# Longer distances, later splits and another block order on a TensorE stream of three blocks (Trainium2, one core)

## The chip, the cores and the metric

The kernel runs on one core of one Trainium2 chip, in one launch. The metric is the device time in microseconds (us), from three runs; one further execution is profiled. Five engines share the work, each with a program order of its own: TensorE (PE in the rows, with PEld for its weight loads), VectorE (DVE), ScalarE (ACT), GpSimd (POOL), and SyncE (SP), which issues most DMAs. TensorE's clock has two levels here, 1.2 and 2.4 GHz; the profile states which one was granted.

## The reference, cut to what matters

256 tokens of width 1024 in float32 go through an even layer, an odd layer and a second block with a mixer and a feed-forward part. Heads are kept 128 or 64 wide.

```python
# even: gated short convolution beside a gated delta rule with 8 heads
g = -exp(a_log) * softplus(a_raw + dt_bias)            # per token and head
decay = exp(where(incl, gc[..., :, None] - gc[..., None, :], -inf))     # gc = cumsum(g) in a chunk
low = where(strict, (kb @ k.T) * decay, 0)
u, w = triangular_solve(low + I, [v * beta, kb * exp(gc)])
o = rms_norm(gated_delta_rule(...), gdn_norm_g) * silu(z_b)
s = concatenate([y_a, o]) @ w_out                      # 16 blocks of 128 rows
# odd: hgrn2 recurrence, s = (rms_norm(o) * silu(z)) @ w_out
# end of both layers, the gate:
x = layer_norm(ALPHA * x + s)
x = x + (p @ w_pl) * sigmoid(x @ w_pl_gate)
# mixer of the second block
y_fox, y_moba = softmax attention (6 + 6 heads of 64, with decay or slopes as bias)
h_ml = mlstm(...)                                      # 4 heads of 64
y_ml = rms(h_ml) * ml_h_g * sigmoid(mo)
x = x + g1 * (concatenate([y_fox, y_ml, y_moba]) @ w_out)
# then the feed-forward part: x + g2 * ((silu(gate) * up) @ w_down)
```

## The kernel before, in words

**Weights.** All large weights lie in one DRAM stream in the order in which TensorE takes them, cut into chunks of 1 MB (16 blocks of 128x128, `BLK`). `Stream` loads a chunk into one of three `raw` buffers (a DMA on SyncE's queue) and splits each half of it in two: ScalarE casts the high part (`hi<-raw`, 128x1024), VectorE subtracts it (`lo<-raw,hi`). There are six buffers each of hi and lo, three chunks in all. `Stream.take` hands TensorE one block after the other, and `fetch` is called from it at each half chunk for the half two chunks ahead. A block costs three matmuls: hi by the high part of the activations, hi by their low part, lo by the high part (`products`, and `dense_tok` for the mixer's values with 512 columns).

**Order.** The order of TensorE's program is written by hand. Everything that isn't a stream of weight blocks (heads of the delta rule, attention pairs, norms) is a generator in a `Side` queue. After every second block, `products` calls `side.tick(0.65)`; a generator that has yielded a number d is resumed d later on that clock, so d sets how many dense blocks stand on TensorE between two steps of a head (0.65 is two blocks: six matmuls of 256 columns, or three of 512 in `dense_tok`). The other engines' orders are made by the framework's scheduler from the same program; an instruction waits in its engine's queue for everything ahead of it. `issue_after` (the `late` argument) keeps a split behind a named instruction in that order.

**Steps that the change touches.**
- `gates` of the delta rule: for each head two tiles `gm` (VectorE scales the constant `gt` by a column of g), read by TensorE with the constant `tri`; ScalarE's exponential gives `la`.
- `gdn_out`, the step of a head: levels m16 and m32 of the inverse with the tiles T, U, MT and X, and at the end the norm, `o` scaled by ScalarE, `yield 4.0`, two transposes of `o`, and y with its split `yh`, `yl`, which the layer's out product reads.
- `out_plan`: the order of (k, m) blocks of an out product; the last four k go bank by bank (a bank is two m). When a bank is full, x is updated and its transposes for the layer norm are queued.
- `layer_tail`'s gate, `GATE_PLANS`: six columns m, then column 6, then column 7. When a bank is full, a tanh, a product (`q<-q,f` in the odd layer) and the add (`x<-x,q`) follow; in the odd layer `fold` transposes x for the next norm.
- the mixer's attention pairs (`pr` is the softmax, transposed after `yield 4.95`) and its `mlstm` (`lo_` is its output, transposed after `yield 4.0`; this `lo_` isn't a weight's `lo`).

Of the kernel before, what the change touches and what calls it, by code (L numbers as in the profile page):

```python
# [6 lines left out]
F32 = mybir.dt.float32  # L7
# [4 lines left out]
ALU = mybir.AluOpType  # L12
# [4 lines left out]
P = 128  # L17
# [13 lines left out]
BLK = 16  # L31
# [29 lines left out]
def out_plan(ks, tail):  # L61


    n = len(ks) - tail
    return [(k, m) for k in ks[:n] for m in range(8)] + \
        [(k, m) for j in range(4) for k in ks[n:] for m in (2 * j, 2 * j + 1)]

# [2 lines left out]
QK_BLOCKS = [0, 1, 6, 7, 2, 3, 8, 9, 4, 5, 10, 11]  # L72

OUT_PLANS = [out_plan([0, 1, 2, 3, 4, 5, 6, 8, 9, 10, 11, 7, 12, 13, 14, 15], 4),
             out_plan(list(range(16)), 4), out_plan([3, 4, 0, 1, 2, 5, 6, 7], 4)]
DOWN_GROUPS = [[0, 1], [2, 3], [4, 5], [6], [7]]

# [28 lines left out]
class Side:  # L106
# [3 lines left out]
    def __init__(self):  # L110
        self.now, self.qs = 0.0, {}
# [36 lines left out]
class Stream:  # L148
# [2 lines left out]

    def __init__(self, net, dram):
        self.net, self.dram, self.n, self.have, self.pos = net, dram, dram.shape[0], {}, 0
        self.late = ()
        self.fetch(0)

    def fetch(self, c, halves=(0, 1), late=()):
        if c < self.n:
            if 0 in halves:
                self.have[c] = self.net.load_chunk(self.dram[c])  # L160
            for h in halves:
                self.net.split_half(self.have[c], h, late)

    def take(self, width=1):
        c, b = divmod(self.pos, BLK)
        self.pos += width
        if c == 0 or c < TWO:
            if b == (0 if c else BLK // 2):
                self.fetch(c + 1, late=() if c else None)
        elif c == TWO:  # L170
            if b % (BLK // 2) == 0:
                self.fetch(c + 1 + b // (BLK // 2))
        else:
            if b % (BLK // 2) == 0:
                self.fetch(c + 2, (b // (BLK // 2),), self.late)
            if b >= BLK // 2:
                self.late = ()
        if b == 0:
            self.have.pop(c - 1, None)
        _, hi, lo = self.have[c]  # L180
        h, j = divmod(b, BLK // 2)
        s = slice(j * P, (j + width) * P)
        return hi[h][:, s], lo[h][:, s]
# [16 lines left out]
class Net:  # L200
# [222 lines left out]
    def gdn_gates(self):  # L423
        nc, ep, pr = self.nc, self.ep, self.prm
        out = self.ps("m")
        mul = self.narrow(self.wba, out)
        for k in range(KT):
            mul(k)
        yield 1.0
        bv = yield from self.to_tokens(out, self.e1, "t1", 0.0)  # L430
        tl = lambda n, w=16: ep.tile([P, w], F32, name="gg_" + n)
        v3 = lambda t: t.rearrange("p (h n) -> p h n", h=2)
        self.beta = tl("beta")
        asp = tl("asp")
        self.tt(v3(asp), bv[:, :, 8:], pr["dt_bias"].unsqueeze(1).to_broadcast([P, 2, 8]), ALU.add)
        th = tl("th")
        self.act(v3(th), bv[:, :, :8], AF.Tanh, scale=0.5)
        self.ts(self.beta, th, 0.5, 0.5)
        sp = self.softplus(self.e1, asp, 16)
        ea = tl("ea", 8)  # L440
        self.act(ea, pr["a_log"], AF.Exp)
        g = tl("g")
        self.stt(v3(g), v3(sp), -1.0, ea.unsqueeze(1).to_broadcast([P, 2, 8]))
        yield 3.5
        q = self.ps("m")
        self.mm(q[:, :16], self.c("tri"), g)
        self.mm(q[:, 16:32], self.c("gt"), g)
        self.eg = ep.tile([P, 32], F32, name="eg")
        self.act(self.eg, q[:, :32], AF.Exp)

        for h in range(0, GH, 2):
            la = ep.tile([P, 2, 2, 2, P], F32, tag="la", bufs=GH // 2, name=self.nm("la"))
            d = self.ps("m")
            for e in range(2):
                gm = self.e1.tile([P, 2, P], F32, tag="gm", bufs=2, name=self.nm("gm"))
                for s in range(2):
                    self.ts(gm[:, s], self.c("gt"), v3(g)[:, s, h + e:h + e + 1])
                    o = d[:, (2 * e + s) * P:(2 * e + s + 1) * P]
                    self.mm(o, gm[:, s], self.c("tri"), stop=False)
                    self.mm(o, self.bf["id"], self.bf["neg"], start=False)  # L460
            self.act(la[:, :, :, 1], d.rearrange("p (e a t) -> p e a t", e=2, a=2), AF.Exp)
            self.la += [la[:, 0], la[:, 1]]
# [143 lines left out]
    def gdn_out(self, h, s, ti, at):  # L606
        nc, ep = self.nc, self.ep
# [13 lines left out]
        for lev in ("m16", "m32"):  # L621
            mt = t2([P, 2, P], "MT")
            self.tt(mt, la[:, :, 0], self.c(lev).unsqueeze(1).to_broadcast([P, 2, P]))
            yield 1.3
            p = self.ps("m")
            for a_ in range(2):
                self.mm(p[:, a_ * P:(a_ + 1) * P], mt[:, a_], t[:, a_])
            self.act(xs, sp(p[:, :T]), AF.Copy)
            yield 0.65
            p2 = self.ps("m")  # L630
            for a_ in range(2):
                if lev == "m32":
                    self.mm(p2[:, a_ * P:(a_ + 1) * P], u[:, a_], xs[:, a_])
                self.mm(p2[:, T + a_ * P:T + (a_ + 1) * P], xs[:, a_], u[:, a_])
            v = p2.rearrange("p (w a t) -> p w a t", w=2, a=2)
            if lev == "m32":
                self.tt(t, t, v[:, 0], ALU.subtract)
            self.tt(u, u, v[:, 1], ALU.subtract)
            if lev == "m16":
                nc.vector.transpose(flat(t), flat(u))  # L640
# [50 lines left out]
        self.stt(sr, sr, P ** -0.5, rr[:, 2:4])  # L691
        for a_ in range(2):
            self.act(o[:, a_], o[:, a_], AF.Copy, scale=sr[:, a_:a_ + 1])
        yield 4.0
        pt = self.ps("m")
        for a_ in range(2):
            self.tr(pt[:, a_ * P:(a_ + 1) * P], o[:, a_])
# [24 lines left out]
    def out_ln_gate(self, i, y, done, lp):  # L722
        nc, xp = self.nc, self.xp
# [29 lines left out]
        for j in range(4):  # L753
            b = self.ps()
# [9 lines left out]
            nh, nl = self.xs()  # L764
        for plan in GATE_PLANS:
            first = plan[0][1]
            n = min(len({m for _, m in plan}), 2)
            bs = [self.ps() for _ in range(3 if n == 2 else 1)]

            def gated(q):  # L770
                j, b = first + 2 * q, bs[q]
                th, pj = gth[:, j // 2 % 2, j % 2:j % 2 + n], pw[j // 4][:, j % 4:j % 4 + n]
                v = x[:, j:j + n]
                self.act(th, b[:, :n * T].rearrange("p (m t) -> p m t", m=n), AF.Tanh, scale=0.5)
                self.stt(th, th, 1.0, pj, ALU.add, ALU.mult)
                self.tt(v, v, th, ALU.add)
                if i == 0:

                    for hs in (slice(0, P), slice(T - 1, P - 1, -1)):
                        self.split(nh[:, j:j + n, hs], nl[:, j:j + n, hs], v[:, :, min(hs.start, P):][:, :, :P])  # L780
                else:
                    self.fold(j, n)
            self.products((xh, xl), [(k, m - first) for k, m in plan], [(b, c) for b in bs for c in (0, T)], self.normed, gated)

    def ln_stats(self, x, j, st):
        yield 1.0
        tp = self.ps("m")
        for a_ in range(2):
            for m in range(2):
                self.tr(tp[:, (2 * a_ + m) * P:(2 * a_ + m + 1) * P], x[:, 2 * j + m, a_ * P:(a_ + 1) * P])  # L790
        for a_ in range(2):
            self.nc.vector.bn_stats(st[:, a_, j], tp[:, a_ * T:(a_ + 1) * T])
        self.banks += 1
# [427 lines left out]
    def softmax_pair(self, p_, kq, vs, yh, yl):  # L1221

        nc, ep = self.nc, self.ep
# [3 lines left out]
        for e in range(2):  # L1227
            h = 2 * p_ + e
            rows = slice(64 * e, 64 * e + 64)
            q, k = kq[rows, p_], kq[rows, 6 + p_]  # L1230
# [10 lines left out]
            s = self.ps("m")  # L1241
# [11 lines left out]
            pts.append(pr)  # L1253
            if e == 0:
                yield 0.65
        yield 4.95
        pt2 = []
        for e in range(2):

# [9 lines left out]
        for e in range(2):  # L1269
            h = 2 * p_ + e  # L1270
# [6 lines left out]
        n = p_ if p_ < 3 else p_ + 2  # L1277
# [34 lines left out]
    def lstm(self, vs, yh, yl):  # L1312
        nc, ep = self.nc, self.ep
# [6 lines left out]
        for h in range(4):  # L1320
            rows = slice(64 * (h % 2), 64 * (h % 2) + 64)
            q, k = self.mqk[rows, h // 2], self.mqk[rows, 2 + h // 2]
            e = self.ps("m")
            for a_ in range(2):
                c = slice(2 * a_ * P, (2 * a_ + 1) * P)
# [6 lines left out]
            s = self.ps("m")  # L1332
# [6 lines left out]
        for a_ in range(2):  # L1339
            pn = self.ps("m")  # L1340
            for h in range(4):
                c = slice(65 * h, 65 * h + 65)
# [5 lines left out]
            v = pn[:, :260].rearrange("p (h d) -> p h d", d=65)  # L1348
# [11 lines left out]
            self.tt(o, o, rs.unsqueeze(2).to_broadcast([P, 4, 64]))  # L1360
            os.append(o)
            yield 0.65
        yield 4.0
        pt = self.ps("m")
        for a_ in range(2):
            for j in range(2):
# [132 lines left out]
```

## Time and profile before

| | us |
|---|---|
| median of three runs (lowest, highest) | 1008.61 (1007.92, 1011.15) |
| the profiled execution's own time | 1007.96 |
| its span from the first to the last instruction | 1006.1 |
| TensorE busy | 978.8 (97%) |
| VectorE busy | 759.1 (75%) |
| ScalarE busy | 554.2 (55%) |
| mean granted clock of TensorE | 0.996 of 2.4 GHz |

A busy share is an average over stages. Matmuls are pipelined, so the duration of one in a row is longer than the distance to the start of the next. "[0.71 <-DVE x L322]" behind a row means that the engine sat idle for 0.71 us before it and what ended that.

### The profile page before, as it was taken

To read this page: it belongs to the slowest core of one execution; us is meant where nothing else is said; L and a number is where in the kernel's file an instruction comes from. 1 tells how busy PE (TensorE), PEld (TensorE's weight loads), DVE (VectorE), ACT (ScalarE), POOL (GpSimd) and SP (SyncE) were. 2 spreads that over 40 slices of the span, in tenths; PEclk is the share of its full clock that TensorE was granted. 3 is DMA by queue.
4 is the path that set the end of the run, shared out by engine and by line. 5 is a ranking of instruction groups with operands and counts; after the bars stand their busy time and mean duration, and the time that the engine had idled before them with its cause. 6 is when DMAs were issued, how large, how long until landed. Compare 5 with 4: busy or idle time off the path is not lost. (4 is left out here: it accounts for less than half of the span.)

```text
span 1006.1 us, 19098 instructions
## 1 busy us (share of the span) xinstructions
PE 978.8 (97%) x7622; PEld 935.6 (93%) x7622; DVE 759.1 (75%) x1459; ACT 554.2 (55%) x1098; POOL 49.9 (5%) x59
## 2 busy tenths in 40 slices
PE   6999999999999999999999999999999999999998
PEld 5999999999999999998989999997777999999998
DVE  5888876888667979889797986889577597665542
ACT  6765556644553864554545534677456674444430
POOL 1000000000000000000000000000223000000000
PEclk9999999999999999999999999999989999999999
DMA  7545523445553595655556563364323547654540
GB/s 283 191 147 177 169 86 126 166 164 177 200 195 126 185 374 208 222 201 201 210 192 230 185 215 132 111 231 135 116 84 126 189 148 272 221 199 168 185 172 22
DMA packets 34617, 179.52 MB, mean 178 GB/s; under 512 B 7648, under 2 KB 8672, under 8 KB 16608
## 3 DMA queue, kind: packets, MB, share of 16 engines
q1 hardware_dynamic: 34096, 177.71, 49.8%
q8 instruction: 60, 0.98, 0.4%
q10 hardware_dynamic: 432, 0.59, 0.2%
q14 instruction: 29, 0.24, 0.1%
HBM read 176.97 MB, written 1.31 MB: 177 GB/s over the span
## 5 line engine op out<-in xcount | busy, mean ns | idle before, releaser
L226 DVE TENSOR_TENSOR lo<-raw,hi 128x1024 fp32r<-128x1024 f32 x280 | 340.6, 1221 | 122.5 <-ACT hi L226 121.8
L226 ACT CAST hi<-raw 128x1024 fp32r<-128x1024 f32 x280 | 292.0, 1047 | 228.3 <-PE psd L312 217.6
L312 PE MATMUL psd<-xh,hi 128*128 128x256 f32 (+1 forms) x1296 | 375.6, 290 | 0.5 <-ACT hi L226 0.5
L312 PE MATMUL psd<-xl,hi 128*128 128x256 f32 (+1 forms) x1296 | 366.7, 283 | 0.4 <-DVE xl L331 0.4
L312 PE MATMUL psd<-xh,lo 128*128 128x256 f32 (+1 forms) x1296 | 366.2, 283 | 0.8 <-DVE lo L226 0.8
L312 PEld LDWEIGHTS psd<-xl,hi 128*128 128x128 f32 x1296 | 245.5, 189 | 1.4 <-DVE xl L331 1.0
L312 PEld LDWEIGHTS psd<-xh,hi 128*128 128x128 f32 x1296 | 245.0, 189 | 1.8 <-ACT hi L226 0.8
L312 PEld LDWEIGHTS psd<-xh,lo 128*128 128x128 f32 x1296 | 245.5, 189 | 1.0 <-DVE lo L226 1.0
L312 PE MATMUL psd<-yh,hi 128*128 128x256 f32 x448 | 130.6, 291 | 0.4 <-ACT yh L334 0.2
L312 PE MATMUL psd<-yl,hi 128*128 128x256 f32 x448 | 126.3, 282 | 1.2 <-DVE yl L235 1.0
L312 PE MATMUL psd<-yh,lo 128*128 128x256 f32 x448 | 126.6, 283 | 0.0
L312 PEld LDWEIGHTS psd<-yl,hi 128*128 128x128 f32 x448 | 84.8, 189 | 1.8 <-DVE yl L235 1.2
L312 PEld LDWEIGHTS psd<-yh,hi 128*128 128x128 f32 x448 | 84.7, 189 | 1.9 <-issue 0.8
L312 PEld LDWEIGHTS psd<-yh,lo 128*128 128x128 f32 x448 | 83.9, 187 | 0.0
L312 PE MATMUL psd<-hi,xh 128*128 128x512 f32 x144 | 60.9, 423 | 0.5 <-DVE lsrc L322 0.5
L1011 DVE SCALAR_TENSOR_TENSOR wa<-wa,cr 128x1024 f32<-128x1024 f32 x48 | 58.4, 1218 | 3.3 <-DMA wa<-in_w_ada_dram 2.7
L312 PE MATMUL psd<-hi,xl 128*128 128x512 f32 x144 | 57.9, 402 | 0.0
L312 PE MATMUL psd<-lo,xh 128*128 128x512 f32 x144 | 57.6, 400 | 0.0
L312 PE MATMUL psd<-al,hi 128*128 128x256 f32 x176 | 49.8, 283 | 0.0
L312 PE MATMUL psd<-ah,lo 128*128 128x256 f32 x176 | 49.7, 283 | 0.0
L312 PE MATMUL psd<-ah,hi 128*128 128x256 f32 x176 | 49.3, 280 | 0.0
L334 ACT ACTIVATE kp<-k 128x512 f32<-128x512 f32 x28 | 19.0, 679 | 33.0 <-DVE k L322 26.2
(338 smaller groups left out, 1397.8 us busy)
## 6 DMA issues: line engine op xcount, KB each, us to landing
raw<-in_w_dram SPq DMA_DIRECT2D x140, 1024.0 KB, 4.8
wa<-in_w_ada_dram SPq DMA_DIRECT2D x48, 512.0 KB, 4.5
cr<-in_c_dram SPq DMA_DIRECT2D x3, 512.0 KB, 5.7
out_dram<-fo SPq DMA_DIRECT2D x3, 256.0 KB, 2.1
cst<-in_cst_dram SPq DMA_DIRECT2D x1, 580.0 KB, 8.3
x<-in_xT_dram ACTq DMA_DIRECT2D x2, 256.0 KB, 4.0
x<-in_xT_dram SPq DMA_DIRECT2D x2, 256.0 KB, 4.8
lev<-in_lev_dram SPq DMA_DIRECT2D x1, 508.0 KB, 4.0
```

The lines of the kernel that those rows point to most:

```text
L226: for i in self.nc.scalar.copy(hi, r), self.nc.vector.tensor_tensor(lo, r, hi.bitcast(F32), ALU.subtract):
L312: self.nc.tensor.matmul(out, lhsT, rhs, start=start, stop=stop, skip_group_check=True, **k)
L334: return self.nc.scalar.activation(out, a, f, bias=bias, scale=scale, **k)
L1011: self.tc.keep_in_program_order(nc.vector.scalar_tensor_tensor(w, w, 1.0, c, ALU.mult, ALU.mult, accum_out=self.md(j)[:, i % 8:i % 8 + 1]))
```

## The change

The output stays the same; the changes are in the order of the work.

```diff
 def out_plan(ks, tail):
     n = len(ks) - tail
-    return [(k, m) for k in ks[:n] for m in range(8)] + \
-        [(k, m) for j in range(4) for k in ks[n:] for m in (2 * j, 2 * j + 1)]
+    bank = lambda ks, j: [(k, m) for k in ks for m in (2 * j, 2 * j + 1)]
+    return [(k, m) for k in ks[:n] for m in range(8)] + bank(ks[n:-2], 0) + bank(ks[n:-2], 1) + \
+        bank(ks[-2:], 0) + bank(ks[-2:], 1) + bank(ks[n:], 2) + bank(ks[n:], 3)
...
+    def release(self, late):
+        held, self.held = self.held, None
+        for h in held:
+            self.fetch(*h, late)
...
-            if b % (BLK // 2) == 0:
+            if b % (BLK // 2) == 0 and self.held is None:
                 self.fetch(c + 2, (b // (BLK // 2),), self.late)
+            elif b % (BLK // 2) == 0:
+                self.held.append((c + 2, (b // (BLK // 2),)))
...
+        def decays(h):
+            gm = self.e1.tile([P, 2, P], F32, tag="gm", bufs=2, name=self.nm("gm"))
+            for s in range(2):
+                self.ts(gm[:, s], self.c("gt"), v3(g)[:, s, h:h + 1])
+            return gm
+        first = [decays(h) for h in range(2)]
         yield 3.5
...
-                gm = self.e1.tile([P, 2, P], F32, tag="gm", bufs=2, name=self.nm("gm"))
+                gm = decays(h + e) if h else first[e]
                 for s in range(2):
-                    self.ts(gm[:, s], self.c("gt"), v3(g)[:, s, h + e:h + e + 1])
...
-            yield 1.3
+            yield 1.95 if h < 4 and lev == "m32" else 1.3
...
-        yield 4.0
+        yield 5.2 if h < 4 else 4.0
         pt = self.ps("m")
         for a_ in range(2):
             self.tr(pt[:, a_ * P:(a_ + 1) * P], o[:, a_])
...
         for plan in GATE_PLANS:
             first = plan[0][1]
+            if first == 6:
+                self.w.held = []
...
-                self.tt(v, v, th, ALU.add)
+                self.end = nc.vector.tensor_tensor(v, v, th, ALU.add)
...
+        self.w.release((self.end,))
...
-        yield 4.95
+        yield 5.85
         pt2 = []
...
-        yield 4.0
+        yield 9.75
         pt = self.ps("m")
         for a_ in range(2):
             for j in range(2):
```

What the edits do to the engines' orders is seen at three places.

VectorE at the start of the even layer, from the last step of the gates' softplus on: lo_223 and lo_227 (after: lo_229 and lo_233) are the low halves of a weight chunk, each gm is a head's decays. Before:

```order
L226 TENSOR_TENSOR lo_223<-raw_220,hi_222 128x1024
L226 TENSOR_TENSOR lo_227<-raw_220,hi_226 128x1024
L326 TENSOR_SCALAR gm_261<-cst,gg_g 128x128 x2
L326 TENSOR_SCALAR gm_268<-cst,gg_g 128x128 x2
L331 SCALAR_TENSOR_TENSOR t_51_327<-psd_156,prm,t_51_327 128x255
L326 TENSOR_SCALAR gm_278<-cst,gg_g 128x128 x2
```

After:

```order
L336 TENSOR_SCALAR gm_208<-cst,gg_g 128x128 x2
L336 TENSOR_SCALAR gm_211<-cst,gg_g 128x128 x2
L236 TENSOR_TENSOR lo_229<-raw_226,hi_228 128x1024
L236 TENSOR_TENSOR lo_233<-raw_226,hi_232 128x1024
L336 TENSOR_SCALAR gm_278<-cst,gg_g 128x128 x2
L336 TENSOR_SCALAR gm_285<-cst,gg_g 128x128 x2
```

The decays of heads 0 and 1 now stand ahead of the two lo; those of heads 2 and 3 stand behind them, as before.

VectorE at the end of the odd layer's gate: x_80 is the activations, q_6945 a gate column's product, xl_7705 the low part for the next projection. Before:

```order
L322 TENSOR_TENSOR x_80<-x_80,q_6945 128x512
L331 SCALAR_TENSOR_TENSOR q_6945<-q_6945,f_6947 128x256
L226 TENSOR_TENSOR lo_7958<-raw_7914,hi_7957 128x1024
L331 SCALAR_TENSOR_TENSOR xl_7705<-x_80,am,xh_7704 128x256 x2
L322 TENSOR_TENSOR x_80<-x_80,q_6945 128x256
L226 TENSOR_TENSOR lo_8013<-raw_8010,hi_8012 128x1024
L331 SCALAR_TENSOR_TENSOR xl_7705<-x_80,am,xh_7704 128x256
L331 SCALAR_TENSOR_TENSOR q_6945<-q_6945,f_6947 128x256
L226 TENSOR_TENSOR lo_8057<-raw_8010,hi_8056 128x1024
L322 TENSOR_TENSOR x_80<-x_80,q_6945 128x256
```

After:

```order
L794 TENSOR_TENSOR x_80<-x_80,q_6945 128x512
L341 SCALAR_TENSOR_TENSOR q_6945<-q_6945,f_6947 128x256
L341 SCALAR_TENSOR_TENSOR xl_7705<-x_80,am,xh_7704 128x256
L794 TENSOR_TENSOR x_80<-x_80,q_6945 128x256
L341 SCALAR_TENSOR_TENSOR xl_7705<-x_80,am,xh_7704 128x256 x2
L341 SCALAR_TENSOR_TENSOR q_6945<-q_6945,f_6947 128x256
L794 TENSOR_TENSOR x_80<-x_80,q_6945 128x256
L236 TENSOR_TENSOR lo_7990<-raw_7987,hi_7989 128x1024
L341 SCALAR_TENSOR_TENSOR xl_7705<-x_80,am,xh_7704 128x256
L236 TENSOR_TENSOR lo_7994<-raw_7987,hi_7993 128x1024
```

No lo stands between a column's product and its add any more; those lo stand behind the last add.

TensorE in the mixer, where the mLSTM's output is transposed (each of the two rows with lo__ is two transposes; psd rows are dense matmuls of the mixer's values, ag_cs and kq rows belong to the first attention pair). Before:

```order
L312 MATMUL psd_8599<-hi_8480,xl_7705 128x512
L312 MATMUL psd_8599<-lo_8481,xh_7704 128x512
L315 MATMUL psm_8684<-cst,lo__1398_8591 128x128 x2
L315 MATMUL psm_8684<-cst,lo__1409_8626 128x128 x2
L312 MATMUL psd_8600<-hi_8480,xh_7704 128x512
```

After:

```order
L325 MATMUL psm_8808<-cst,ag_cs 128x128 x2
L322 MATMUL psm_8814<-kq_8423 128x128
L322 MATMUL psm_8814<-kq_8423 128x256
L322 MATMUL psd_8774<-hi_8603,xh_7704 128x512
L322 MATMUL psd_8774<-hi_8603,xl_7705 128x512
L322 MATMUL psd_8774<-lo_8604,xh_7704 128x512
L325 MATMUL psm_8849<-cst,lo__1398_8591 128x128 x2
L325 MATMUL psm_8849<-cst,lo__1409_8626 128x128 x2
```

The four transposes moved behind 27 dense matmuls of 512 columns (nine blocks' worth of `dense_tok`), eight transposes of `sq`, and the bias and score matmuls of the first two pairs of score steps.

## Rows read from the trace of the kernel before

**Rows 1.** The page's busy times (part 1: busy us, share, instructions).

```profile
PE 978.8 (97%) x7622; PEld 935.6 (93%) x7622; DVE 759.1 (75%) x1459; ACT 554.2 (55%) x1098; POOL 49.9 (5%) x59
```

**Rows 2.** The page's chain (part 4) and costliest groups (part 5).

```profile
PE psd L312 21%; PE psm L312 1%; PE psm L315 0%; DVE xl L331 0%; DVE mt L331 0%; DVE lo L226 0%; DVE fo L331 0%; DVE al L235 0%; DVE fu L322 0%; DVE ft L331 0%; DVE shc L1079 0%
...
L226 ACT CAST hi<-raw 128x1024 fp32r<-128x1024 f32 x280 | 292.0, 1047 | 228.3 <-PE psd L312 217.6
```

**Rows 3.** TensorE's waits, whole span: us in total, times, longest.

```profile
PE psm L315 <- DVE lo__1398_8591 L322: 1.8, 1, 1.8
...
PE psm L315 <- DVE lo__1409_8626 L322: 1.6, 1, 1.6
PE psm L315 <- DVE x L322: 1.5, 2, 0.8
...
PE psm L315 <- DVE pr L326: 1.3, 2, 1.1
PE psd L312 <- DVE yl L235: 1.0, 1, 1.0
...
PE psm L315 <- ACT kv L334: 0.6, 1, 0.6
```

**Rows 4.** Timeline of VectorE at the gates: start, us, instruction, count.

```profile
17.55 2.35 DVE L226 TENSOR_TENSOR lo<-raw,hi 128x1024 fp32r<-128x1024 f32 x2
19.82 0.86 DVE L326 TENSOR_SCALAR gm<-cst,gg_g 128x128 f32<-128x128 f32 x4
...
21.02 0.48 DVE L326 TENSOR_SCALAR gm<-cst,gg_g 128x128 f32<-128x128 f32 x2
```

**Rows 5.** Timeline of TensorE at the gates, heads 0 and 2.

```profile
20.16 0.49 PE L312 MATMUL psm<-cst,gm 128*128 128x128 f32 x2 [1.69 <-DVE gm L326]
...
21.53 0.44 PE L312 MATMUL psm<-cst,gm 128*128 128x128 f32 x2
```

**Rows 6.** Timeline of ScalarE ahead of the first delta head.

```profile
32.55 1.28 ACT L334 ACT_TABLE_LOAD   x1
```

**Rows 7.** Timeline of TensorE in a delta head below 4.

```profile
128.02 0.68 PE L312 MATMUL psm<-T,MT 128*128 128x128 f32 x4 [0.70 <-DVE T L640]
...
133.46 0.41 PE L312 MATMUL psm<-T,la 64*64 64x64 f32 x4 [0.44 <-ACT X L334]
...
150.94 0.28 PE L312 MATMUL psd<-xh,lo 128*128 128x256 f32 x1
151.06 0.38 PE L315 MATMUL psm<-cst,o 128*128 128x128 f32 x2
152.32 0.62 PE L315 MATMUL psm<-cst,o 128*128 128x128 f32 x2 [0.88 <-ACT o L334]
```

**Rows 8.** Timeline of VectorE in the same head.

```profile
131.76 1.22 DVE L226 TENSOR_TENSOR lo<-raw,hi 128x1024 fp32r<-128x1024 f32 x1
...
149.09 1.22 DVE L226 TENSOR_TENSOR lo<-raw,hi 128x1024 fp32r<-128x1024 f32 x1
```

**Rows 9.** Timeline of VectorE in the even out product.

```profile
301.81 1.22 DVE L226 TENSOR_TENSOR lo<-raw,hi 128x1024 fp32r<-128x1024 f32 x1
```

**Rows 10.** Busy time by window: odd gate's end, next projection, mixer's values (PE, PEld, DVE, ACT, POOL; clock).

```profile
655.00:667.40 12.40, 11.00 (x92) 10.59 (x90) 12.39 (x21) 10.85 (x30) 0.00 (x0) 1.00 0.69 245
667.43:684.92 17.49, 17.13 (x139) 16.35 (x140) 14.12 (x33) 12.21 (x24) 0.87 (x3) 1.00 0.51 177
720.77:726.62 5.85, 5.85 (x26) 4.42 (x25) 4.23 (x16) 2.18 (x4) 2.31 (x2) 1.00 0.47 179
725.00:750.00 25.00, 21.57 (x91) 15.83 (x90) 17.44 (x66) 12.20 (x34) 4.55 (x3) 0.86 0.13 45
730.79:737.47 6.68, 6.68 (x22) 5.26 (x21) 3.57 (x6) 1.84 (x3) 0.00 (x0) 0.63 0.46 157
```

**Rows 11.** Timeline of SyncE's queue at the even gate's end.

```profile
352.18 0.36 SPq L215 DMA_DIRECT2D raw<-in_w_dram  x1
```

**Rows 12.** The tile `raw` from 340 to 370 us, its six loads.

```profile
DMA to landing us min/median/max: 4.7/7.7/9.4
```

More of the change, by code (lines that the diff above doesn't have):

```diff
@@ L153, in __init__ @@
         self.net, self.dram, self.n, self.have, self.pos = net, dram, dram.shape[0], {}, 0
+        self.held = None
         self.late = ()
```

## The prediction

> **What bounds the kernel now.** I read the page's busy times first: TensorE works 978.8 us, 97% of the span, VectorE 75% and ScalarE 55% [rows 1]. The chain that ended last says the same, TensorE's dense matmuls ahead of all else, and of ScalarE's idle time before its casts 217.6 of 228.3 us ended when TensorE let a buffer go [rows 2]. So the split weights wait for TensorE, not the reverse, and a microsecond taken from TensorE's program at one place isn't waited out at the next place by default. What can be won is TensorE's idle time, 1006.1 - 978.8 = 27.3 us, and time at a lower clock. Next I read TensorE's waits, longest first [rows 3]: the mLSTM's output, the odd gate's x, the attention's pr, the out product's yl and a head's kv. The gates' gm has 1.69 us [rows 5], heads below 4 have 0.70, 0.44 and 0.88 us [rows 7]. These lie at the places that the edits touch: 1.69 + 0.6, 2.0, 1.0, 1.5, 3.4 and 1.3 make 11.5 us. Every edit moves instructions and adds or takes away no work of note, so its worth is the wait there, less the wait that takes its place. Last I read VectorE beside each of these waits, to see what stood in its queue.
>
> **Gates.** VectorE ran two lo, 2.35 us, ahead of the first gm at 19.82 [rows 4]. With the four gm (0.86 us) ahead, TensorE's first pair of heads can start when it arrives, 20.16 - 1.69 = 18.47. A pair lasts 21.53 - 20.16 = 1.37 us [rows 5], so it is done at 19.84. But the second pair's gm still stand behind both lo: 17.55 + 0.86 + 2.35 = 20.76, where they began at 21.02 [rows 4]; TensorE can read the first of them some 0.3 us later, as at 20.16 after 19.82. The second pair then starts at 21.06 and not at 21.53: of 1.69 us 0.47 is won, and 1.2 becomes a new wait for gm. That is the working case; if the later pairs' gm and the convolution's steps between them come faster or slower, it is between 0.3 and 1.7. Behind it, the first head's kv was late by 0.6 us [rows 3], right behind a table load of 1.28 us on ScalarE [rows 6]. The changed order puts the exponentials of `la` together and ahead of the first silu, so that load goes; I take 0.55, between 0 and 0.6. Sum: -1.0, bounds -0.3 and -2.3.
>
> **Heads 0 to 3.** 1.95 for 1.3 puts one more tick, six matmuls, ahead of T,MT: 6 x 0.12 = 0.72 us (150.94 to 151.06 is the distance of two matmuls [rows 7]) against a wait of 0.70. The copy X for the next step now follows a split on ScalarE; I charge 0.3 for it. The 0.44 us at 133.46 is named after X, but this is the second head's matmul, and its T was computed behind the lo at 131.76 [rows 8], which the new order puts elsewhere: 0.44 won. Before the transposes of o, 5.2 for 4.0 puts six to twelve more matmuls, 0.7 to 1.5 us, against 0.88, and the lo at 149.09 no longer stands inside the norm [rows 8]: 0.88 won. Other heads of the four have no wait to lose, and could get one; I charge 0.2. Sum 0.70 - 0.3 + 0.44 + 0.88 - 0.2 = 1.5; bounds -0.7 (X late by all it can be, and a wait in each other head) and -2.0 (no charge).
>
> **Out product.** The last two k, those of the last heads, are first read after both banks' other blocks: two k by two m more, 12 matmuls or 1.45 us later, than in the old order. The wait for yl, 1.0 us [rows 3], behind a lo at 301.81 [rows 9], is covered. Bank 0 is full 12 matmuls later, so its update of x and its transposes come later beside a lo; charge 0.2. The odd layer has no such wait, and the charge could appear there too. Sum -0.8, bounds 0 and -1.0.
>
> **Gate's end.** In the odd layer VectorE is busy for 12.39 of 12.40 us before the end [rows 10], and the lo between product and add delay x: 1.5 us in two waits [rows 3]. Held splits take four lo out, by the order. They don't vanish: 4 x 1.17 = 4.7 us come into the next stretch, which has 17.49 - 14.12 = 3.4 us of idle VectorE [rows 10]. Starting 1.5 earlier, VectorE is through with the next projection's xl at -1.5 + 4.7 - 3.4 = -0.2, while TensorE would be 1.5 earlier. So most of the wait moves to xl. TensorE's own idle there, 17.49 - 17.13 = 0.36 [rows 10], is swallowed by it: -0.2 - 0.36 = -0.6. Bounds +0.3 (the release in one piece also delays a cast in front of xh) and -1.5. In the even layer there is no wait to win. There the held chunk's load moves on SyncE's queue behind lev, cr and two wa, to where a chunk went out at 352.18 [rows 11]. With the longest landing near there, 9.4 us [rows 12], it is in by 361.6, split by 363.8 (a cast of 1.05 [rows 2], a lo of 1.22 [rows 8]); TensorE wants it at about 368, my estimate from its place in the order. The cover is 4 us; I take 0.
>
> **Mixer.** The mLSTM's transposes wait 1.8 + 1.6 us [rows 3], with VectorE's two lo_ behind a norm. 9.75 for 4.0 moves them behind 27 dense matmuls; 24 of these took 5.85 us at full clock [rows 10], so 27 take 6.6, more than 3.4 plus the first transposes' 0.4. Both waits go: -3.4. After them the clock fell: 0.63 in the 6.68 us of the next 18 dense matmuls, 1.00 in the stretch ahead [rows 10]; the lower of the two levels, 1.2 GHz, after two idle stretches close together. At full clock these 18 cost 18 x 5.85 / 24 = 4.39 us, so the fall cost 2.3. Without the idle I expect no fall: -2.3. The page "TensorE: Matmul & The Clock Gate" of the Trainium skill, section "HAM oscillation — how this bites in real kernels", charges half of the throttled time. By the mean of 0.86 over 725 to 750 us that is 25 x 0.14 = 3.5 us, and the sum would be 1.2 us better; part of that stretch had no matmul to slow down, so the 2.3 from the dense rows stands. The attention's 5.85 for 4.95 puts six 512-column matmuls, 1.46 us, ahead of the transposes of pr, whose waits are 0.2 and 1.1 [rows 3]: -1.3. The mLSTM's last steps now run beside the first pair's softmax on VectorE and ScalarE; charge 0.3. Sum -6.7; bounds -4.1 (no clock regained, charge doubled) and -7.0.
>
> **Sum.** -1.0 - 1.5 - 0.8 - 0.6 - 6.7 = -10.6, from the profiled run's own 1007.96 to 997.4. The median of the three runs stands 0.65 higher, which gives 998.0; I forecast 997.7. The ends add to -4.8 (1003.2) and -13.8 (994.2).
>
> **Rivals.**
> *The waits only move.* Orders on VectorE are fixed, and each place above gets new company: the gates show it (1.2 of 1.69 comes back), the odd gate too. For it: VectorE's full stretch before the gate's end. Against it: 75% overall. With every term at its low end the time is 1003.2. Chance 0.25.
> *The clock still falls in the mixer.* Small matmuls and transposes stand where dense ones stood, so short idle pieces may do what two long ones did. Then 2.3 us stay: 997.7 + 2.3 = 1000.0. Against it: the fall followed 3.4 us of idling with four transposes between, and none of the waits left [rows 3] is near that. The page "TensorE: Matmul & The Clock Gate" of the Trainium skill, section "A second HAM failure mode: psum-queue depth-cycling", says that frequent short idling between groups of matmuls makes the clock swing; no run here shows it yet. Chance 0.06.
> *Slower: the late chunk at the even gate.* TensorE stands still from 368 us until it is split. It decides from a landing at 368 - 2.3 + 10.6 = 376.3 on, 24 us after its issue, where the time is 1008.3, and each us more costs one; a landing at 380 gives 1012. With the longest landing of 9.4 us [rows 12] its issue would have to slip from 352.18 [rows 11] to beyond 367. Chance 0.04.
> *Nothing is won.* TensorE's gaps are pipeline shadows, or what is saved is lost further on to the weight stream: 1008 within 3 us. The 217.6 us of rows 2 speak against it. Chance 0.05.
>
> **How the numbers follow.** The forecast has 0.60 and by itself spans 995.5 to 1000. About 0.3%, 3 us, can be told from no change here. Faster takes the forecast, the clock's case and nearly all of the moved waits: 0.60 + 0.06 + 0.24 = 0.90. Same takes the last rival and the worst of the first, 0.06; slower 0.04. The range is 994 to 1003: it leaves out the last two rivals and the upper part of the first, some 0.19.
>
> **What would show it.** In the changed kernel's trace: a wait for gm of about 1.2 us at the second pair; no wait for lo_, pr and yl; a granted clock of 1.00 from 720 to 745; new waits for xl after the odd gate; no wait for hi or lo near 360 us. The prediction is wrong if the clock falls in the mixer, if waits for X, kq or o grow in heads or pairs that had none, or if the end of the odd gate costs more than before.

## The result and the profile after

| | before | changed |
|---|---|---|
| median (executions) | 1008.26 us (4) | 998.25 us (4) |
| lowest | 1007.28 | 996.74 |
| profiled execution's own time, span | 1007.96, 1006.1 | 998.75, 996.9 |
| mean granted clock in the profiled execution | 0.996 | 0.998 |

The ratio is 0.9891, 95% interval 0.9863 to 0.9919: about 10 us, 1.1%, faster. One of the four executions of the changed kernel ran at a mean clock of 0.56 and took 1570 us; the median of 998.25 counts it, the ratio leaves it out, and the other three took 996.74, 997.74 and 998.75.

The page's busy times of the changed kernel, part 1, answer to [rows 1]:

```profile
PE 977.0 (98%) x7622; PEld 935.7 (94%) x7622; DVE 758.1 (76%) x1459; ACT 551.3 (55%) x1096; POOL 52.1 (5%) x59
```

TensorE's idle time fell from 27.3 to 19.9 us; its busy time fell by 1.8, while its mean clock rose from 0.996 to 0.998. TensorE's waits in the changed kernel, whole span, answer to [rows 3] (us in total, times, longest):

```profile
PE psm L322 <- ACT xh L244: 4.6, 1, 4.6
PE psm L322 <- DVE T L656: 2.8, 3, 1.2
PE psm L325 <- POOL mss L1047: 1.9, 1, 1.9
...
PE psm L322 <- DVE gm L336: 1.2, 1, 1.2
PE psd L322 <- DVE xl L341: 0.8, 2, 0.6
...
PE psm L322 <- DVE kq L1232: 0.3, 1, 0.3
PE psm L325 <- ACT o L344: 0.3, 1, 0.3
```

lo_, x, pr, yl and kv are gone from the list. Behind the wait for the first xh at the start, which the kernel before has too (4.7 us), T and the norm's mss now stand ahead.

Where each part of the 9.2 us between the two profiled executions came from is seen by the same dense matmul in both timelines of TensorE (there are as many in each, in the same order). The output step of heads 2 and 3 comes only behind the mark of heads 0 to 3; it has no wait in either kernel.

| first dense matmul behind | before, us | changed, us | step |
|---|---|---|---|
| the gates' matmuls and the first kv | 36.01 | 34.94 | -1.07 |
| heads 0 to 3 | 180.03 | 180.36 | +1.40 |
| heads 4 to 7 | 298.10 | 297.84 | -0.59 |
| the even out product's end | 310.14 | 308.44 | -1.44 |
| (odd layer, up to its out product) | 655.10 | 653.63 | +0.23 |
| odd gate and the next projection | 700.18 | 698.24 | -0.47 |
| the mixer | 800.00 | 790.82 | -7.24 |

Behind the mixer nothing is given back: the difference is still 9.2 us at the end.

**Gates.** VectorE (first fence) and TensorE (second) in the changed kernel, against [rows 4, 5]:

```profile
17.84 0.88 DVE L336 TENSOR_SCALAR gm<-cst,gg_g 128x128 f32<-128x128 f32 x4
18.63 2.36 DVE L236 TENSOR_TENSOR lo<-raw,hi 128x1024 fp32r<-128x1024 f32 x2
20.89 0.88 DVE L336 TENSOR_SCALAR gm<-cst,gg_g 128x128 f32<-128x128 f32 x4
```

```profile
18.49 0.47 PE L322 MATMUL psm<-cst,gm 128*128 128x128 f32 x2
...
21.23 0.49 PE L322 MATMUL psm<-cst,gm 128*128 128x128 f32 x2 [1.23 <-DVE gm L336]
```

The first pair starts when TensorE arrives, and the wait comes back one pair later.

**Heads 2 and 3.** VectorE, then TensorE, then the busy time and clock behind the waits (PE, PEld, DVE, ACT, POOL; clock), changed kernel:

```profile
156.82 1.22 DVE L236 TENSOR_TENSOR lo<-raw,hi 128x1024 fp32r<-128x1024 f32 x1
157.95 0.48 DVE L341 SCALAR_TENSOR_TENSOR t<-psd,prm,t 128x255 f32<-128x255 f32 x1
158.34 0.41 DVE L332 TENSOR_TENSOR U<-U,psm 128x256 f32<-128x256 f32 x1
158.67 0.47 DVE L341 SCALAR_TENSOR_TENSOR t<-psd,prm,t 128x254 f32<-128x254 f32 x1
159.06 0.43 DVE L656 STREAM_TRANSPOSE T<-U 128x256 f32<-128x256 f32 x1
```

```profile
159.65 0.68 PE L322 MATMUL psm<-T,MT 128*128 128x128 f32 x4 [1.23 <-DVE T L656]
161.29 1.19 PE L322 MATMUL psm<-T,MT 128*128 128x128 f32 x4 [0.96 <-DVE T L656]
```

```profile
160.00:165.00 5.00, 4.04 (x22) 3.87 (x22) 3.20 (x7) 1.50 (x4) 0.00 (x0) 0.66 0.33 106
```

U's input was ready at about 156.3, when TensorE was through with U,X (155.22, 1.05 us); a weight's lo and a step t of the convolution stand in front of it in VectorE's fixed order. These heads had no such wait before, and behind the two waits the clock fell to the lower level for some 3 us.

**Odd gate.** GpSimd behind the last add, in the kernel before and in the changed one, then VectorE and TensorE of the changed one:

```profile
671.06 0.69 POOL L339 TENSOR_TENSOR mrs<-ms,mhalf 128x2 f32<-128x2 f32 x1 [3.35 <-DVE ms L1062]
```

```profile
667.51 3.88 POOL L349 TENSOR_TENSOR mrs<-ms,mhalf 128x2 f32<-128x2 f32 x1 [3.65 <-DVE ms L1081]
```

```profile
667.27 0.16 DVE L1081 TENSOR_REDUCE ms<-mss 128x2 f32<-128x12 f32 x1
667.34 3.49 DVE L236 TENSOR_TENSOR lo<-raw,hi 128x1024 fp32r<-128x1024 f32 x3
```

```profile
671.44 0.43 PE L325 MATMUL psm<-cst,mrs 128*128 128x128 f32 x2 [1.86 <-POOL mss L1047]
...
679.12 0.38 PE L322 MATMUL psd<-xl,hi 128*128 128x256 f32 x1 [0.60 <-DVE xl L341]
```

The two waits for x (1.5 us) are gone. In their place TensorE waits for the norm's factor mrs, a power of two numbers per partition on GpSimd that takes 3.88 us; the same instruction took 0.69 us in the kernel before, at 671.06. (The matmul reads mrs; its row names mss, a memset that GpSimd does right behind the power.) The power now runs beside three lo on VectorE.

**Mixer.** Busy time and clock of the changed kernel, against the windows of [rows 10]:

```profile
725.00:735.00 10.00, 9.67 (x49) 7.04 (x47) 7.53 (x30) 5.70 (x16) 3.56 (x3) 1.00 0.31 105
735.00:745.00 10.00, 9.77 (x48) 7.35 (x47) 7.82 (x37) 5.88 (x18) 2.79 (x2) 1.00 0.00 0
```

TensorE is busy for 19.4 of 20 us, at full clock.

### The profile page after: what moved, and what is told of

The parts are those of the page before. It is cut to its first block, busy times and chain, and to the rows that moved or that the text cites. A ratio compares the mean times of both kernels' runs of the same rounds, so it can differ in the third digit from the quotient of the medians.

```text
span 996.9 us, 19085 instructions
## 1 busy us (share of the span) xinstructions
PE 977.0 (98%) x7622; PEld 935.7 (94%) x7622; DVE 758.1 (76%) x1459; ACT 551.3 (55%) x1096; POOL 52.1 (5%) x59
## 4 chain that ended last, share of the span: by engine, by line
PE 81%; DVE 10%; ACT 4%; DMA 2%; issue 2%; POOL 1%; SPq 0%; ACTq 0%; POOLq 0%; DVEq 0%
PE psd L322 67%; PE psm L322 11%; DVE lo L236 3%; PE psm L325 3%; ACT hi L236 2%; DMA raw<-in_w_dram 1%; DVE q L332 1%; DVE k L332 1%; DVE at L959 1%; DVE wa L1030 1%; DMA ti<-dti 1%; POOL mrs L349 0%; DVE xl L341 0%; ACT xh L344 0%; DVE t L341 0%
## 5 line engine op out<-in xcount | busy, mean ns | idle before, releaser
L344 ACT ACTIVATE kp<-k 128x512 f32<-128x512 f32 x28 | 19.0, 678 | 33.0 <-DVE k L332 27.3
```

The lines of the kernel that those rows point to most:

```text
L344: return self.nc.scalar.activation(out, a, f, bias=bias, scale=scale, **k)
```

## The experiments

Theory: each edit wins the wait at its place, and what it costs is what its new place has in VectorE's queue. Three things had to be told apart: which delay brought the waits of heads 2 and 3, why the power took 3.88 us, and what the clock hangs on. Differences behind a place are those of the same dense matmul in the profiled executions, as in the table above. They carry noise of their own: the transfer of ti, a tile of the heads' inverse, landed 4.8 to 7.1 us after its issue in the thirteen profiled executions. Where it took 6.3 us or more (e3, e4, e5, e6, e8), TensorE has one more wait for T, 0.4 or 0.5 us near 120 us, and passes heads 0 to 3 some 0.6 to 1.7 us later than the nearest kernel with the same heads, though none of these edits touches them.

**e1: the heads' output distance alone.** In the changed kernel:

```diff
-            yield 1.95 if h < 4 and lev == "m32" else 1.3
+            yield 1.3
```

> The changed kernel with the longer distance before T,MT taken back (1.3 for 1.95), the longer one before the transposes of o kept. Theory (only both delays together bring heads 2 and 3 to where a weight's lo stands ahead of U on VectorE): their two waits for T, 1.2 and 1.0 us, and the fall of the clock behind them go, 0.7 and 0.4 us come back in heads 0 and 1; TensorE is 2 to 2.5 us earlier behind the heads than in the changed kernel, about 996 to 997 us. Rival (the later output step alone pushes y and its splits in front of U): the waits of 1.2 and 1.0 stay, no gain, 998 to 1000 us.

**e2: the distance before T,MT alone.**

```diff
-        yield 5.2 if h < 4 else 4.0
+        yield 4.0
```

> The changed kernel with the output distance taken back to 4.0, 1.95 before T,MT kept. Theory as above: the two waits of heads 2 and 3 go and with them the fall of the clock, 0.9 us comes back before the transposes of o in heads 0 and 1; TensorE is 2 to 3 us earlier behind the heads, about 996 us. Rival (1.95 alone makes heads 2 and 3 meet the convolution's three steps and a lo): one or both waits stay, 998 us or more.

Measured: e1 997.80 us median (996.82 to 999.76), e2 997.35 (996.43 to 999.58). Behind heads 0 to 3, at the dense matmul of 180.03 in the kernel before, TensorE was 2.7 us (e1) and 3.3 us (e2) ahead of the changed kernel's profiled execution, in which the clock fell. Against e10 below, the same program at full clock, it is 1.0 and 1.6 us: that is what the waits cost, and the rest goes with the fall. TensorE's waits from 100 to 170 us in e1:

```profile
PE psm L322 <- DVE T L656: 0.5, 1, 0.5
PE psm L322 <- ACT X L344: 0.4, 1, 0.4
PE psm L325 <- ACT o L344: 0.2, 1, 0.2
```

The waits of heads 2 and 3 are gone with either delay, and in e2 no wait is left in this stretch at all; the 0.9 us for o, expected back, didn't come. So it was the two delays together, as the theory had it. In both kernels VectorE's order has both U ahead of the next lo again. The medians lie above what was expected and differ from the changed kernel's by less than its executions spread; the gain stands on the traces.

**e3: splits not held.** The lines with `held = []` and `release` are taken out of the changed kernel.

> The changed kernel without the held splits. Theory (holding trades the two waits for x, 1.5 us, for one of 1.9 us for the norm's factor and 0.6 for xl, and wins only what stood in the next stages): those two go, 0.7 and 0.8 us before the transposes of x come back, and by the change's own measured step at this place (0.5 us) TensorE is 0.3 to 0.7 us later behind the odd gate; total within 1 us of the changed kernel. Rival (the hold is what wins at the odd gate, as forecast 0.6 and up to 1.5): 1 us or more later.

Measured: 998.54 us (997.52 to 1000.78). TensorE's waits from 650 to 690 us in e3:

```profile
PE psm L325 <- DVE x L792: 1.5, 2, 0.8
PE psd L322 <- DVE lsrc L332: 0.5, 1, 0.5
PE psd L322 <- DVE xl L341: 0.4, 1, 0.4
```

From 655.10 to 688.88 this kernel loses 0.14 us to the one before, and the changed kernel gains 0.46: the hold is worth 0.6 us, as forecast, with the power's wait already paid. Here heads 2 and 3 had the same two waits, 1.23 and 0.96 us, but behind them the clock stayed (busy time and clock from 160 to 166):

```profile
160.00:166.00 6.00, 4.64 (x38) 4.51 (x39) 5.58 (x14) 2.36 (x7) 0.00 (x0) 1.00 0.31 91
```

**e4: the mixer's two distances on the kernel before.**

```diff
-        yield 4.95
+        yield 5.85
...
-        yield 4.0
+        yield 9.75
```

> The kernel before with the two distances of the mixer alone (9.75 and 5.85). Theory: the two waits for lo_ and those for pr go and the clock stays at 2.4 GHz from 720 to 745 us without any help of the other edits: 6.7 to 7.3 us below the kernel before, about 1001 us. Rival (the fall of the clock hangs on more than these two waits): granted clock still under 1.00 there, 4.4 us below before, about 1004 us.

Measured: 1002.54 us (1000.01 to 1002.74), ratio 0.9930, 0.9904 to 0.9955. Busy time and clock from 720 to 745, and TensorE's waits from 715 to 780:

```profile
720.00:745.00 25.00, 24.45 (x120) 18.61 (x120) 18.82 (x76) 13.21 (x35) 7.77 (x5) 1.00 0.24 85
```

```profile
PE psm L312 <- DVE kq L1213: 0.3, 1, 0.3
PE psm L315 <- DVE bias L322: 0.2, 1, 0.2
```

TensorE passes the mixer 7.2 us faster than before, as much as in the changed kernel and without any help of the other edits.

**e5: lo kept away from the power.** On e2, VectorE copies the factor right behind the power, and the next lo are queued behind that copy:

```diff
         self.rsqrt(rs, s2)
+        if self.which == 0:
+            self.w.late, self.w.keep = (self.nc.vector.tensor_copy(t1([P, 2], "msm"), rs),), True
         yield 3.9
+        self.w.late, self.w.keep = (), False
...
-            if b >= BLK // 2:
+            if b >= BLK // 2 and not self.keep:
                 self.late = ()
```

> The kernel of e2 in which the lo of the next half chunks after the odd gate are queued on VectorE behind a small copy that reads the norm's factor mrs, so that no lo runs beside GpSimd's power on 128x2. Theory (the power took 3.9 us for 0.7 because three lo, with both inputs in SBUF, ran beside it): the power takes 0.7 us again and TensorE's wait for the factor, 2.0 us, goes or falls below 0.3; VectorE idles about 1 us and the three lo then make xl later, so behind the projection TensorE is 0.3 to 1.2 us earlier than in e2. Rival (GpSimd is slow there for another reason, such as a cold start of its code): the power still takes 3 us or more and, with the lo behind it, TensorE loses 2 to 3 us more.

Measured: 994.24 us (993.60 to 994.78), ratio 0.9840, 0.9817 to 0.9862. GpSimd, VectorE and TensorE of e5:

```profile
665.84 0.70 POOL L350 TENSOR_TENSOR mrs<-ms,mhalf 128x2 f32<-128x2 f32 x1 [3.65 <-DVE ms L1082]
```

```profile
666.57 0.17 DVE L1085 COPY msm<-mrs 128x2 f32<-128x2 f32 x1 [0.53 <-POOL mrs L350]
666.65 3.49 DVE L237 TENSOR_TENSOR lo<-raw,hi 128x1024 fp32r<-128x1024 f32 x3
```

```profile
667.65 0.38 PE L326 MATMUL psm<-cst,mrs 128*128 128x128 f32 x2
...
672.92 0.38 PE L323 MATMUL psd<-xl,hi 128*128 128x256 f32 x1 [0.43 <-DVE xl L342]
```

The power takes 0.70 us again after the same 3.65 us of idling, so a cold start isn't the cause; the three lo beside it are. TensorE doesn't wait for mrs. From 655.10 to 688.88 the kernel gains 1.62 us on the one before, against 0.35 in e2: 1.27 of the 2.0 us wait is won, and of the rest 0.5 is seen at xl (1.1 us in two waits, against 0.6 in e2). The late ti cost this profiled execution 1.7 us against e2 in heads 0 to 3, which the edit doesn't touch.

**e6: the second lo behind the last decays.** On e2, the second half of that chunk is split behind the last gm:

```diff
-                self.fetch(c + 1, late=() if c else None)
+                self.fetch(c + 1, (0, 1) if c else (0,), late=() if c else None)
...
             self.la += [la[:, 0], la[:, 1]]
+        self.w.fetch(1, (1,), (self.last_gm,))
```

> The kernel of e2 with the second lo at the gates queued behind the last decays; the first lo stays behind the first four. Theory (the 1.2 us that came back is the second pair's gm behind two lo): with one lo there the wait falls to 0.0 to 0.2 us, TensorE is 1.0 to 1.2 us earlier behind the gates than in e2, and the late lo, needed 3 us after the gates, is covered. Rival (the later pairs are bound by VectorE's gm and the convolution's steps anyway): 0.5 us or less.

Measured: 997.41 us (994.75 to 999.49). TensorE's timeline in e6, first and second pair:

```profile
20.04 0.47 PE L322 MATMUL psm<-cst,gm 128*128 128x128 f32 x2
...
21.40 0.44 PE L322 MATMUL psm<-cst,gm 128*128 128x128 f32 x2
```

The second pair follows the first without a wait. The profiled execution was itself no faster than e2's: its clock was already lower in the start (0.84 from 14 to 20 us) and fell behind the power's wait (0.57 from 671 to 675), and ti landed late. So the edit's worth is seen in the rows, 1.2 us, and in e7, not in this median: from the dense matmul at 11.88 in the kernel before to that at 36.01, e7 is 1.15 us faster than e2.

**e7: e5 and e6 together on e2.**

> The edits of e5 and e6 together on e2. If both theories hold, their gains add, since they lie 640 us apart: 1.3 to 2.4 us below e2's span, 992.2 to 993.3 us. If the lock isn't the cause, it ends above e2's span of 994.6 less the gates' 1.1.

Measured: 992.47 us (991.47 to 992.68), ratio 0.9822, 0.9803 to 0.9841; the span is 990.9, shorter than expected. Behind the gates and the first kv it is 2.00 us ahead of the kernel before (e2 1.43), the odd gate gains 1.56. Another 0.8 us comes behind the mixer, in the feed-forward part, where TensorE's order is that of e2. It isn't a wait: between the dense matmuls of 935 and 990 us in the kernel before, they start 118.8 ns apart on the mean in the four traces with e5's edit (e5, e7, e9, e11) and 120.0 in the other nine. Why isn't settled.

**e8: the mLSTM's transposes two ticks later.** On the kernel before, 5.3 for 4.0.

> The kernel before with 5.3 for 4.0 ahead of the mLSTM's transposes: six dense matmuls, 1.46 us, ahead of them. Their first wait falls from 1.85 to 0.4 us, the second stays at 1.6. Theory (the clock falls behind two long idle stretches close together and not behind one): granted clock 1.00 from 725 to 745, 1.46 + 2.3 = 3.8 us below before. Rival (one wait of this size is enough): it falls again, 1.5 us below before.

Measured: 1006.08 us (1004.09 to 1009.40), ratio 0.9969, 0.9955 to 0.9984. TensorE's waits from 730 to 740, and busy time and clock in three windows:

```profile
PE psm L315 <- DVE lo__1409_8626 L322: 1.6, 1, 1.6
PE psm L315 <- DVE lo__1398_8591 L322: 0.4, 1, 0.4
```

```profile
732.00:735.00 3.00, 1.27 (x7) 0.97 (x8) 1.85 (x5) 0.00 (x0) 1.01 (x1) 1.00 0.02 5
735.00:738.00 3.00, 3.00 (x9) 2.32 (x8) 2.85 (x6) 1.66 (x3) 0.00 (x0) 0.50 0.55 167
738.00:742.00 4.00, 4.00 (x23) 2.92 (x22) 1.98 (x9) 2.60 (x7) 0.00 (x0) 0.95 0.33 137
```

Neither holds as put. In the profiled execution the clock went to the lower level with 0.4 and 1.6 us of waiting too, 0.50 for three microseconds, and TensorE passed this stretch (720.77 to 745.04 in the kernel before) only 2.2 us faster. But four of the ten executions had a mean clock of 1.000, and of the 27 executions of the kernel before beside the experiments one. So by this count, of whole executions, the shorter wait makes the fall rarer; it doesn't end it.

**e9: 1.95 in all heads,** on e7 (`if lev == "m32"` without `h < 4`).

> The kernel of e7 with 1.95 before T,MT in all eight heads. Theory (a distance pays where T is late at its place and VectorE's order keeps): the wait of 0.6 us for T in heads 6 and 7 goes, heads 4 and 5 have none to lose: 0.4 to 0.7 us below e7's span of 990.9. Rival (as in heads 2 and 3 before: the shift brings T behind other work of VectorE): a wait of 0.5 us or more stays or a new one comes, and the span is that of e7 or longer.

Measured: 992.93 us (991.88 to 994.98), span 990.1. The wait for T in heads 6 and 7 went, and that for o grew from the 0.4 us (once) of e7, as TensorE's waits from 160 to 300 show:

```profile
PE psm L326 <- ACT o L345: 1.2, 2, 0.7
```

The span of the profiled execution is 0.8 us shorter and the median 0.5 higher than e7's: undecided, and in any case less than one wait's worth.

**e10 and e11: the changed kernel and e7 on one chip.**

> The changed kernel once more, on the same chip as e9 and e11, to see how often its clock falls. If the waits of 1.9 us (norm's factor) and 1.2 plus 1.0 us (heads 2 and 3) only sometimes lower the clock, its executions spread over 2 us or more and their mean clocks over 0.997 to 1.000, while e11's stay within 1.5 us.

> The kernel of e7 once more beside the changed kernel on one chip: 5 to 6 us below it, all executions within 1.5 us of each other, mean clock 1.000 in all.

Measured: the changed kernel 999.02 us (997.07 to 1001.10), clocks 0.996 to 1.000; e7 992.42 us (992.28 to 993.00), clock 1.000 in all four. e7 beats both kernels, the changed one by 6.6 us here, 0.6 more than expected.

In e10's profiled execution TensorE has the same waits as in the changed kernel (1.23 and 0.96 us in heads 2 and 3, 1.9 for the factor), and the clock stayed (busy time and clock, against the row of heads 2 and 3 above):

```profile
160.00:165.00 5.00, 4.04 (x35) 3.97 (x35) 4.61 (x11) 1.97 (x6) 0.00 (x0) 1.00 0.37 118
```

It passes heads 0 to 3 with a step of -0.16 us where the table above has +1.40, and took 997.07 us.

## Why the prediction was right, and which step was not

997.7 was forecast, 998.25 measured. By terms, profiled execution against profiled execution (the sum gave 997.4 for it, and it took 998.75):

| term | forecast | measured |
|---|---|---|
| gates | -1.0 | -1.07 |
| heads 0 to 3 | -1.5 (-0.7 to -2.0) | +1.40 |
| heads 4 to 7 | 0 | -0.59 |
| even out product | -0.8 (0 to -1.0) | -1.44 |
| gate's end | -0.6 | -0.47 |
| mixer | -6.7 | -7.24 |

**Gates:** right in size and place, 0.42 us won at the gates (0.47 forecast) and 0.8 at kv (0.55); the wait of 1.2 us for gm came back at the second pair, and the table load of [rows 6] no longer stands before kv. e6 shows that it is the second lo.

**Heads:** the step that failed is "Other heads of the four have no wait to lose, and could get one; I charge 0.2". The waits at heads 0 and 1 went as worked out: e2, with one of the two distances and no other wait in their place, has -1.56. But in the changed kernel heads 2 and 3 got 1.23 and 0.96 us, and in this execution a fall of the clock behind them, so the term was 2.9 us off and outside its bounds. By e10, with the same waits and no fall, 1.3 of that are the waits and 1.6 the fall. e1 and e2 show that neither delay alone does it; each moved heads 2 and 3 on TensorE, and VectorE's order, made anew, put a lo and the convolution's step in front of U. The order of the changed kernel shows this, and the charge should have been taken from there.

**Out product:** mis-sized by 0.6, outside its bounds. The waits for yh and yl went whole, 1.2 us together, and the charge of 0.2 for bank 0 didn't come.

**Gate's end:** the sum was right by luck, the wait named was not. I had it at xl; it is the norm's factor (1.86 us), xl has 0.60. What held lo do to GpSimd had no place in the term, though the trace of the kernel before shows it (last section). e3 confirms the 0.6 for the hold; e5 shows that without the lock it is worth about 1.6. Nothing waited for the held load at the even gate, so the rival of the late chunk had no part in it.

**Mixer:** right, and 0.2 beyond its bounds. The waits of 3.4 and 1.3 us and the fall of the clock (2.3) are gone, less 0.6 us of new waits for kq and bias against a charge of 0.3; e4 gives the same 7.2 alone. That makes 6.4. The other 0.8 is seen at pr: from the first of its twelve transposes to the dense matmul behind them TensorE took 1.82 and 2.68 us before and 1.23 and 1.28 now, 2.0 us less for waits of 1.3. The row of the matmul in front of a wait reaches into it, so the idle time of a row is less than what the wait costs. The rival of a clock that still falls was wrong for this place, but right elsewhere: it fell behind heads 2 and 3.

The total was right partly by luck: heads (2.9 us worse) were made up in part by heads 4 to 7, the out product and the mixer (1.8 us better); what is left, 1.4 us, lies within the range. Of the signs of being wrong that the prediction named, one came, a wait for kq (0.33 us) in a pair that had none, about the size of the charge; the waits that grew in the heads are for T, which it didn't name. Heads 4 to 7 had no term: no edit touches them, and their smaller waits came with VectorE's new order. That is seen, not tested.

## What to carry to other kernels

A longer distance for one wait moves everything behind it on the clock of the order: read in the new order of the other engines what stands in front of the next late tile, for every head that the number touches. A wait isn't won before it is known what its producer waits for next in a fixed queue: one lo put behind the decays and three kept from GpSimd's power took e2 from 997.35 to 992.47 us. And a fall of the clock adds to the price of the wait ahead of it (1.6 us in heads 2 and 3); with the waits behind which it fell removed the executions lay closer together (e5 and e7 within 1.2 us, the changed kernel within 2 to 4), though four executions are few and those of e9 spread over 3.1.

## What the hardware showed

**VectorE's lo holds up GpSimd.** The power on 128x2 took 0.69 or 0.70 us alone (eight traces) and 3.88 us beside three lo (the other five), and ended 0.6 us behind the third: it got hardly a turn between them. In the kernel before, the power on 128x4 took 1.01 us alone and 1.91 beside one lo, as GpSimd's timeline shows:

```profile
725.95 1.91 POOL L339 TENSOR_TENSOR lrs<-lss,mhalf 128x4 f32<-128x4 f32 x1 [1.54 <-DVE lss L328]
728.93 1.01 POOL L339 TENSOR_TENSOR lrs<-lss,mhalf 128x4 f32<-128x4 f32 x1 [1.07 <-DVE lss L328]
```

The page "SBUF — State Buffer" of the Trainium skill, section "Who interferes with whom", says that a VectorE instruction with two SBUF inputs contends with a GpSimd instruction that reads SBUF, and calls this contention for the shared ports an exclusive lock. The traces agree, and e5 shows it by keeping them apart; that three lo in a row shut GpSimd out until the last is what the traces add. A busy VectorE alone doesn't do it: in the kernel before the power on 128x8 took 1.64 us alone (at 717.57), 2.48 where it began beside a lo (750.32) and 1.67 where it began beside VectorE's scaling of pr, one tile by a column (764.98).

**The clock doesn't fall every time.** Behind two waits of 1.23 and 0.96 us it fell in the changed kernel (0.66 from 160 to 165) and not in e3, nor in e10, which is the same program. Behind a single wait for the factor it fell in e1 (1.8 us) and not in e2 (2.0 us). Busy time and clock of e1, then of e2:

```profile
671.00:675.00 4.00, 4.00 (x26) 4.00 (x26) 3.35 (x8) 2.65 (x6) 0.00 (x0) 0.69 0.39 164
```

```profile
671.00:675.00 4.00, 4.00 (x35) 3.95 (x34) 3.56 (x9) 3.94 (x7) 0.00 (x0) 1.00 0.51 207
```

From 673.30 to 683.02 in the kernel before, e1 lost 1.3 us to e2 by it. What decides between the two stays open.
